# Lane steps, row loads and evacuation places of a hybrid encoder layer, on one core

## Chip, core and metric

The kernel runs on one core of one Trainium2 chip. The metric is the device time in microseconds (us) of one execution, as the median over runs. The core's engines are TensorE (PE, with its weight loads PEld), VectorE (DVE), ScalarE (ACT), GpSimd (POOL) and SyncE (SP), which here issues nearly all DMAs.

## The reference

One layer of a bidirectional hybrid encoder, in float32, on two sequences with shared weights: 1024 tokens (sample) and 256 tokens (prompt), 2048 features, each with a memory of 256 rows.

```python
hn = rms_norm(x, norm_g)
proj = hn @ w_in                       # 2048 x 4896
xbc, z_ssd, dt_raw, q, k, v, z_att, mq, z_mem = split_cols(proj, IN_SIZES)
xbc = silu(centred_dwconv(xbc, conv_w, conv_b))          # 5 taps along the tokens
xs, Bm, Cm = split_cols(xbc, (1024, 256, 256))
dt = softplus(dt_raw + dt_bias); A = -exp(a_log)
y = ssd_scan(forward) + ssd_scan(backward) + d_skip * xs  # 16 heads of 64, chunks of 128
o_ssd = rms_norm(y * silu(z_ssd), per group of 512)
o_att = window_attention(rms_norm(q), rms_norm(k), v, sink) * silu(z_att)  # 8 heads of 64, 2 kv heads
mk, mv = split_cols(rms_norm(mem) @ w_mem_kv)
o_mem = softmax(rms_norm(mq) @ rms_norm(mk).T) @ mv * silu(z_mem)          # 4 heads of 128
return x + concat([o_ssd, o_att, o_mem]) @ w_out
```

In a chunk the scan needs exp(acs[i] - acs[j]) for all pairs of tokens i, j, with acs the running sums of dt * A; both directions share one weight matrix per head.

## The kernel before

The 1280 tokens are ten tiles of 128 (tiles 0 to 7 the sample, 8 and 9 the prompt), in two groups of five. The big products run one after the other as blocks: first the memory's keys and values (two blocks of four tiles), then for group 0 the blocks q, kv (with dt), za (gate of the attention), x (six blocks, followed by the convolution), mq, zm, z0 and z1, then group 1 in another order, then the output product for both groups. `block_tok` accumulates five token tiles over 16 slices of the contraction (a step is one slice), `block_feat` two feature chunks in two halves of 320 tokens. Each product is done in three passes on rounded numbers: the activations are kept as a high and a low part (xH, xL), and each weight slice is loaded by SP (wraw, four places), rounded on ScalarE (wh, L219 or L222) and its rest formed on VectorE (wl, L220 or L223), with three places each. When a block's accumulators (five banks, tile acc) are complete, an evacuation function takes them out: `ev_mk`, `ev_raw` and `ev_dtkv` copy through a tile with the tag "evu" (two places) and store to DRAM, the gates use "evt" for the tanh (th) and "evu" for the result (zs), the convolution "evu" for its input and "evt" for the rest.

Everything else is written as generators, the lanes. Two queues of generators take turns; `pump(n)` runs n steps, a step being the code up to the next `yield`. `run` gives a block's rate: so many lane steps per slice (the table RATES, one column for each group). `need` runs steps until a named generator is done. The lanes are: `x_stats` and `mem_stats` (sums of squares of the rows of x and of the memory, tiles xst and mst, then the reciprocal root), `vectors` (small parameters; aneg is -exp(a_log)), `mk_prep`, `k_prep`, `attn` and `mem_attn` (load a tile that an evacuation stored, square it on ScalarE, sum on VectorE, `rsqrt`, multiply on VectorE, transpose on TensorE, then scores and values), `dt_prep` (running sums, stored to the tensor ac), `ssd_up` (forward sweep of the scan, and the weights within a chunk) and `ssd_down` (backward sweep). `rsqrt` is two instructions of GpSimd, L133 (scale and EPS) and L134 (power -0.5).

In `ssd_up`, `weights(q)` makes the weight matrices of four heads: rows of running sums are loaded from ac to all 128 partitions (rf forward, two places; rb backward, three places), ScalarE adds a bias per head (L848, eight instructions), VectorE merges both (copy_predicated, L849), ScalarE takes the exponential (L850) and VectorE multiplies (L851); `diag` uses the matrices on TensorE. The first product of a tile's `ssd_up` is pcb (L775), on the chunks that the convolution stored (bc).

The order on each engine is not the order of the source alone: a scheduler takes instructions by priority (the place in the source; weight splits and evacuations are moved up by high_priority) as soon as it expects their inputs and places to be ready. The queues themselves run in order on the chip.

Of the kernel before, what the change touches and what calls it, by code (L numbers as in the profile page):

```python
# [10 lines left out]
F32 = mybir.dt.float32  # L11
# [8 lines left out]
P = 128  # L20
# [7 lines left out]
SCR = 1024  # L28
CH, WB, RB, WA, WBB = 3, 3, 4, 5, 4
RBB = 3  # L30
RATES = ({'kv': 1.7, 'q': 1.5, 'za': 1.5, 'x': 1.5, 'mq': 2.52, 'zm': 1.8, 'z0': 2.17, 'z1': 1.26},
         {'kv': 0.84, 'x': 1.35, 'z0': 3.81, 'z1': 2.6, 'q': 2.65, 'za': 0.93, 'mq': 2.9, 'zm': 2.54,
          'o': 2.6})
NEG = -1e30

C_X, C_Z, C_DT, C_Q, C_K, C_V, C_ZA, C_MQ, C_ZM = 0, 1536, 2560, 2592, 3104, 3232, 3360, 3872, 4384
# [4 lines left out]
def hymba_encoder_kernel(  # L41
# [24 lines left out]
    ev = ctx.enter_context(tc.tile_pool(name="ev", bufs=2))  # L66
# [65 lines left out]
    def rsqrt(dst, src, scale, n):  # L132
        G.tensor_scalar(out=dst, in0=src, scalar1=scale, scalar2=EPS, op0=ALU.mult, op1=ALU.add)  # L133
        G.tensor_tensor(out=dst, in0=dst, in1=mhalf[:, :n], op=ALU.pow)  # L134
# [201 lines left out]

    def ev_raw(dst, base):
        def f(i, ps):
            z = ev.tile([P, 512], F32, tag="evu", name="qs")
            A.activation(z, ps, AF.Copy)  # L340
            S.dma_start(dst[base + i], z)
        return f

    def ev_dtkv(base):
        def f(i, ps):
            t = base + i
            rt = rx[:, t:t + 1]
            r = ev.tile([P, P], F32, tag="evu", name="kraw")
            A.activation(r, ps[:, 32:160], AF.Copy, scale=rt)
# [56 lines left out]
    def w2(name):  # L406
        return mp.tile([P, 512], F32, tag="wa", name=name, bufs=WA)

    def ev_mk(i, ps):
        kr = ev.tile([P, 512], F32, tag="evu", name="mkr")  # L410
        A.activation(kr, ps, AF.Copy)
        S.dma_start(mq_d[i], kr)

# [8 lines left out]
    def mk_prep(i):  # L422
        kr = w2("mkr")
        S.dma_start(kr, mq_d[i])
        ss = sm.tile([P, 4], F32, tag="s4", name="ss", bufs=4)
        sq = w2("sq")
        rm = rx[:, 10 + i:11 + i]
        A.activation(sq, kr, AF.Square, scale=rm)
        V.reduce_sum(out=ss, in_=hv(sq, 4), axis=AX.X)
        r = sm.tile([P, 4], F32, tag="s4", name="r", bufs=4)  # L430
        rsqrt(r, ss, 1.0 / P, 4)
        V.scalar_tensor_tensor(out=hv(kr, 4), in0=hv(kr, 4), scalar=rm, in1=hb(r, 4, P), op0=ALU.mult, op1=ALU.mult)
        V.tensor_mul(hv(kr, 4), hv(kr, 4), gm.unsqueeze(1).broadcast_to([P, 4, P]))
        for _ in range(4):
            yield
        ps = psum("pmk")
        for h in range(4):
            T.transpose(ps[:, h * P:(h + 1) * P], kr[:, h * P:(h + 1) * P], ident)
        c = slice((i % 2) * P, (i % 2) * P + P)
        if i < 2:  # L440
            A.activation(mkH[:, :, c], hv(ps, 4), AF.Copy)
            V.tensor_sub(mkL[:, :, c], hv(ps, 4), mkH[:, :, c].bitcast(F32))
        else:
            o = w2("mko")
            A.activation(o, ps, AF.Copy)
            S.dma_start(mk_d[:, :, c], hv(o, 4))
        yield
# [13 lines left out]
    def k_prep(t):  # L461
        r = w2("kr")[:, :P]
        S.dma_start(r, k_d[t])
        ss = sm.tile([P, 2], F32, tag="s2", name="kss", bufs=4)
        sq = w2("ksq")[:, :P]
        A.activation(sq, r, AF.Square)
        V.reduce_sum(out=ss, in_=hv(sq, 2), axis=AX.X)
        rr = sm.tile([P, 2], F32, tag="s2", name="krr", bufs=4)
        rsqrt(rr, ss, 1.0 / 64, 2)
        r3 = hv(r, 2)  # L470
        V.tensor_mul(r3, r3, hb(rr, 2, 64))
# [87 lines left out]
    def attn(t):  # L559
# [7 lines left out]
        tc_ = slice(ti * P, (ti + 1) * P)  # L567
        q = w2("q")
        S.dma_start(q, q_d[t])
        sq = w2("sq")  # L570
        A.activation(sq, q, AF.Square, scale=rx[:, t:t + 1])
        ss = sm.tile([P, 8], F32, tag="s8", name="qss", bufs=4)
        V.reduce_sum(out=ss, in_=hv(sq), axis=AX.X)
        r = sm.tile([P, 8], F32, tag="s8", name="qr", bufs=4)
        rsqrt(r, ss, 1.0 / 64, 8)
        q3 = hv(q)
        V.scalar_tensor_tensor(out=q3, in0=q3, scalar=rx[:, t:t + 1], in1=hb(r, 8, 64), op0=ALU.mult, op1=ALU.mult)
        yield
        yield
        yield  # L580
        qT = []
        for b in range(2):
# [12 lines left out]
        z = w2("za")  # L595
# [70 lines left out]
    def mem_attn(t):  # L666
        grp, ti = divmod(t, 5)
        tc_ = slice(ti * P, (ti + 1) * P)
        q = w2("mq")
        S.dma_start(q, mq_d[t])  # L670
        sq = w2("sq")
        A.activation(sq, q, AF.Square, scale=rx[:, t:t + 1])
        ss = sm.tile([P, 4], F32, tag="s4", name="mss", bufs=4)
        V.reduce_sum(out=ss, in_=hv(sq, 4), axis=AX.X)
        r = sm.tile([P, 4], F32, tag="s4", name="mr", bufs=4)
        rsqrt(r, ss, 1.0 / P, 4)
        q3 = hv(q, 4)
        V.scalar_tensor_tensor(out=q3, in0=q3, scalar=rx[:, t:t + 1], in1=hb(r, 4, P), op0=ALU.mult, op1=ALU.mult)
        yield
        yield  # L680
        yield
        ps = psum("pmq")
        for h in range(4):
# [5 lines left out]
        z = w2("zm")  # L689
# [68 lines left out]
    def ssd_up(t):  # L758
# [6 lines left out]
        for g in range(2):  # L765
            x = wb("xc", shape=(P, 4, P))
            S.dma_start(x, xbc_d[4 * g:4 * g + 4, :, tok].rearrange("f p c -> p f c"))
            xc.append(x)
        yield
        yield  # L770
        yield

        ps = psum("pcb")
        for g in range(2):
# [26 lines left out]
        for g in range(2):  # L801
# [22 lines left out]
            if not first:  # L824
# [4 lines left out]
                S.dma_start(sb_d[t][:, c], st)  # L829
                yield  # L830
        mts = {}

        def weights(q):
            g = q // 2

            rf = mp.tile([P, 512], F32, tag="rf", name="rf", bufs=2)
            mt = mp.tile([P, 512], F32, tag="rb", name="rb", bufs=RBB)
            r0 = 32 * (t % 5) + 4 * q
            for d, r in enumerate((rf, mt)):
                S.dma_start(r, ac_d[t // 5][r0 + 16 * d:r0 + 16 * d + 4, :]  # L840
                            .rearrange("h c -> (h c)").partition_broadcast(P))
            yield

            for d, r in enumerate((rf, mt)):
                for j in range(4):
                    c = slice(j * P, (j + 1) * P)
                    h = 16 * d + 4 * q + j
                    A.activation(r[:, c], r[:, c], AF.Identity, bias=wj_all[:, t, h:h + 1])  # L848
            V.copy_predicated(hv(mt, 4), upper.bitcast(U32).unsqueeze(1).broadcast_to([P, 4, P]), hv(rf, 4))  # L849
            A.activation(mt, mt, AF.Exp)  # L850
            V.tensor_mul(hv(mt, 4), hv(mt, 4), cb[:, g, :].unsqueeze(1).broadcast_to([P, 4, P]))  # L851
            mts[q] = mt

        def diag(g):
# [9 lines left out]
            V.tensor_add(ya[g], ya[g], py)  # L864
            S.dma_start(yp_d[t][:, g * 512:(g + 1) * 512], ya[g])

        for q in range(3):
            yield from weights(q)
            yield
        diag(0)  # L870
        yield
        yield from weights(3)
        yield
        yield
        diag(1)
# [136 lines left out]
    def vectors(_):  # L1012
        gk, gmk = w2("gk")[:, :64], w2("gmk")[:, :P]
        for t, a in ((gq, q_norm_g[0]), (gk, k_norm_g[0]), (gm, mq_norm_g[0]), (gmk, mk_norm_g[0]),
                     (dskip, d_skip[0]), (sinkb, sink[0]), (dtb, dt_bias.rearrange("o a h -> (o a h)")),
                     (aneg, a_log.rearrange("o a h -> (o a h)"))):
            S.dma_start(t, a.partition_broadcast(P))
        yield
        yield
        yield  # L1020
        yield
        V.scalar_tensor_tensor(out=gq, in0=gq, scalar=64 ** -0.5, in1=gk, op0=ALU.mult, op1=ALU.mult)
        V.scalar_tensor_tensor(out=gm, in0=gm, scalar=P ** -0.5, in1=gmk, op0=ALU.mult, op1=ALU.mult)
        A.activation(aneg, aneg, AF.Exp)
        V.tensor_scalar(out=aneg, in0=aneg, scalar1=-1.0, scalar2=None, op0=ALU.mult)
        yield
# [153 lines left out]
```

## Time and profile before

| | |
|---|---|
| median of 3 runs | 1917.64 us (1916.83 to 1919.4) |
| profiled execution | 1925.01 us, span 1923.3 us |
| busy | PE 1875.9 us, DVE 1049.4 us, ACT 760.9 us, POOL 81.6 us |
| DMA | 289.40 MB, mean 150 GB/s |

The span is the time from the first to the last instruction in the profiled execution; that execution is the one with the profiler on. A row of the list of instructions in order of time reads: start, length, engine, line, operation, written tile<-read tiles, shapes, count, and in brackets the idle time of the engine just before and what ended it. A row of the list of waits reads: engine, tile and line that waited <- engine, tile and line that it waited for: total us, times, longest. L12 is line 12 of the kernel.

### The profile page before, as it was taken

The page shows a single profiled execution, that of the slowest core. Times are in us where ns is not written, and L with a number is a line of the kernel's source. Part 1 is how long each engine was busy: PE and PEld are TensorE (multiplying, and loading weights), DVE is VectorE, ACT ScalarE, POOL GpSimd, SP SyncE. Part 2 cuts the span into 40 slices and gives each one's busy share as a digit, 9 for nine tenths or more (in the row PEclk, how much of TensorE's full clock was granted, in tenths as well). Part 3 has the DMA queues.
Part 4 walks back from the last instruction along what each step waited for, and adds up shares of the span by engine and source line. Part 5 has one row for each costly group of instructions (what it writes and reads, how often), then busy time and mean ns, then how long its engine had stood idle before and what let it go on. Part 6 is the DMA issues. An engine that isn't in the chain of part 4 may idle for free.

```text
span 1923.3 us, 28675 instructions
## 1 busy us (share of the span) xinstructions
PE 1875.9 (98%) x10568; PEld 1634.2 (85%) x10568; DVE 1049.4 (55%) x2133; ACT 760.9 (40%) x1721; POOL 81.6 (4%) x147
## 2 busy tenths in 40 slices
PE   8999989999999999999999999999999999999999
PEld 6779989998898879999978778978978787778887
DVE  4443646677564555667776554576675454542222
ACT  6462463333452545423436444334453333421121
POOL 1010010000000000000100000000000000000000
PEclk9999999999999999999999999999999999999999
DMA  8683563233343545433444567655555345454432
GB/s 272 198 257 104 157 182 121 85 114 109 116 124 113 154 140 172 138 96 101 140 131 142 158 177 247 209 187 162 170 158 186 123 149 159 136 176 132 133 120 69
DMA packets 191340, 289.40 MB, mean 150 GB/s; under 512 B 18977, under 2 KB 68193, under 8 KB 191201
## 3 DMA queue, kind: packets, MB, share of 16 engines
q1 hardware_dynamic: 191056, 287.53, 48.9%
q8 instruction: 83, 1.36, 0.3%
q14 instruction: 57, 0.46, 0.1%
q10 hardware_dynamic: 144, 0.06, 0.0%
HBM read 230.59 MB, written 56.92 MB: 149 GB/s over the span
## 4 chain that ended last, share of the span: by engine, by line
PE 77%; DMA 11%; ACT 4%; DVE 4%; issue 2%; POOL 1%; SPq 1%; ACTq 0%; DVEq 0%; POOLq 0%
PE acc L269 14%; PE acc L270 14%; PE acc L271 14%; PE acc L304 8%; PE acc L305 8%; PE acc L306 8%; DMA xst<-in_x_sample_dram 2%; DMA rf<-ac 2%; PE po L648 2%; PE py L858 1%; PE ppt L637 1%; DMA rb<-ac 1%; DVE wl L220 1%; PE pst L826 1%; PE pst L817 1%
## 5 line engine op out<-in xcount | busy, mean ns | idle before, releaser
L269 PE MATMUL acc<-wh,xH 128*128 128x512 f32 (+1 forms) x1568 | 619.0, 395 | 9.0 <-ACT wh L219 5.6
L270 PE MATMUL acc<-wl,xH 128*128 128x512 f32 (+1 forms) x1568 | 601.6, 384 | 2.9 <-DVE wl L220 2.7
L271 PE MATMUL acc<-wh,xL 128*128 128x512 f32 (+1 forms) x1568 | 600.3, 383 | 0.0
L220 DVE TENSOR_TENSOR wl<-wraw,wh 128x512 fp32r<-128x512 f32 (+1 forms) x416 | 278.3, 670 | 384.4 <-ACT wh L219 376.1
L219 ACT ACTIVATE wh<-wraw 128x512 fp32r<-128x512 f32 (+1 forms) x416 | 254.1, 612 | 528.7 <-PE acc L271 268.0
L304 PE MATMUL acc<-xH,wh 128*128 128x320 f32 x1280 | 406.1, 317 | 9.0 <-DVE zs L331 4.7
L306 PE MATMUL acc<-xH,wl 128*128 128x320 f32 x1280 | 396.6, 310 | 1.6 <-DVE wl L220 1.4
L305 PE MATMUL acc<-xL,wh 128*128 128x320 f32 x1280 | 396.6, 310 | 0.0
L269 PEld LDWEIGHTS acc<-wh,xH 128*128 128x128 f32 x1568 | 296.4, 189 | 69.2 <-issue 8.4
L270 PEld LDWEIGHTS acc<-wl,xH 128*128 128x128 f32 x1568 | 296.7, 189 | 62.9 <-issue 6.6
L271 PEld LDWEIGHTS acc<-wh,xL 128*128 128x128 f32 x1568 | 296.2, 189 | 56.5 <-issue 0.6
L304 PEld LDWEIGHTS acc<-xH,wh 128*128 128x128 f32 x1280 | 241.3, 189 | 15.0 <-DVE zs L331 5.2
L305 PEld LDWEIGHTS acc<-xL,wh 128*128 128x128 f32 x1280 | 241.3, 189 | 3.3 <-issue 3.2
L306 PEld LDWEIGHTS acc<-xH,wl 128*128 128x128 f32 x1280 | 241.1, 188 | 2.3 <-DVE wl L220 2.3
L223 DVE SCALAR_TENSOR_TENSOR wl<-wraw,vec,wh 128x512 fp32r<-128x512 f32 x64 | 48.0, 750 | 128.0 <-ACT wh L222 128.0
L222 ACT ACTIVATE wh<-wraw,vec 128x512 fp32r<-128x512 f32 x64 | 46.3, 723 | 145.4 <-PE acc L271 132.3
L379 DVE SCALAR_TENSOR_TENSOR c<-u,vec,c 128x638 f32<-128x638 f32 (+1 forms) x96 | 84.5, 880 | 1.0
L848 ACT ACTIVATE rb<-rb,wj_all 128x128 f32<-128x128 f32 x160 | 53.0, 391 | 49.1 <-DMA rb<-ac 46.5
L848 ACT ACTIVATE rf<-rf,wj_all 128x128 f32<-128x128 f32 x160 | 53.6, 390 | 33.5 <-DMA rf<-ac 33.5
L622 ACT ACTIVATE lg<-lg,nm 128x384 f32<-128x384 f32 (+1 forms) x80 | 45.1, 564 | 46.2 <-DVE nm L616 46.1
L849 DVE COPY_PREDICATED rb<-upper,rf 128x512 f32<-128x512 uint32 x40 | 30.3, 757 | 53.0 <-ACT rb L848 52.8
L214 DVE SCALAR_TENSOR_TENSOR xL<-chd,vec,xH 128x640 fp32r<-128x640 f32 (+1 forms) x48 | 39.6, 837 | 23.5 <-ACT xH L213 23.5
(238 smaller groups left out, 1725.5 us busy)
## 6 DMA issues: line engine op xcount, KB each, us to landing
wraw<-in_w_in_laid_dram SPq DMA_DIRECT2D x288, 256.0 KB, 2.8
wraw<-in_w_out_laid_dram SPq DMA_DIRECT2D x128, 256.0 KB, 2.7
chd<-in_x_turned_dram SPq DMA_DIRECT2D x32, 320.0 KB, 4.1
rf<-ac SPq DMA_DIRECT2D x40, 256.0 KB, 3.8
rb<-ac SPq DMA_DIRECT2D x40, 256.0 KB, 4.2
out_dram<-yt SPq DMA_DIRECT2D x40, 256.0 KB, 3.6
wraw<-in_w_mem_laid_dram SPq DMA_DIRECT2D x32, 256.0 KB, 4.3
xst<-in_x_sample_dram SPq DMA_DIRECT2D x32, 256.0 KB, 4.9
```

What stands on the lines that cost most here:

```text
L219: A.activation(h, raw, AF.Copy)
L220: V.tensor_sub(l, raw, h.bitcast(F32))
L222: A.activation(h, raw, AF.Copy, scale=g)
L223: V.scalar_tensor_tensor(out=l, in0=raw, scalar=g, in1=h.bitcast(F32), op0=ALU.mult, op1=ALU.subtract)
L269: T.matmul(ps[t][:, :n], sh, h[:, :n], start=(k_ == 0), stop=False)
L270: T.matmul(ps[t][:, :n], sh, l[:, :n], start=False, stop=False)
L271: T.matmul(ps[t][:, :n], sl, h[:, :n], start=False, stop=(k_ == KT - 1))
L304: T.matmul(o, sh, cur["H", q][:, m, c], start=(k == 0), stop=False)
L305: T.matmul(o, sh, cur["L", q][:, m, c], start=False, stop=False)
L306: T.matmul(o, sl, cur["H", q][:, m, c], start=False, stop=(k == KT - 1))
L379: V.scalar_tensor_tensor(out=c[:, :n], in0=u[:, k:k + n], scalar=cw[k], in1=c[:, :n], op0=ALU.mult, op1=ALU.add)
L848: A.activation(r[:, c], r[:, c], AF.Identity, bias=wj_all[:, t, h:h + 1])
```

## The change

Four things change in the source.

- In `mk_prep`, `k_prep`, `attn` and `mem_attn` a yield is added behind the load, and one or two between `rsqrt` and the multiplication that uses it; yields behind the multiplication are taken out, so that `attn` and `mem_attn` (of which the first is shown) keep their number of steps, `mk_prep` has one more and `k_prep` two. `vectors` waits six steps instead of four for its loads, with one more before the exponential of a_log.
- In `ssd_up` the loads of the rows are taken out of `weights(q)` into `rows(q)`, which is called a step ahead; for tiles 0 and 4 six yields stand behind the first loads instead of three.
- `ev_raw`, `ev_dtkv` and `ev_mk` (the first is shown) take their tile from "evt" for odd tiles and from "evu" for even ones.
- All rates are set anew.

```diff
-RATES = ({'kv': 1.7, 'q': 1.5, 'za': 1.5, 'x': 1.5, 'mq': 2.52, 'zm': 1.8, 'z0': 2.17, 'z1': 1.26},
-         {'kv': 0.84, 'x': 1.35, 'z0': 3.81, 'z1': 2.6, 'q': 2.65, 'za': 0.93, 'mq': 2.9, 'zm': 2.54,
-          'o': 2.6})
+RATES = ({'kv': 1.8, 'q': 1.7, 'za': 1.7, 'x': 1.7, 'mq': 2.7, 'zm': 1.9, 'z0': 2.4, 'z1': 1.6},
+         {'kv': 1.0, 'x': 1.4, 'z0': 3.7, 'z1': 2.8, 'q': 2.8, 'za': 1.3, 'mq': 2.8, 'zm': 2.4,
+          'o': 2.65})
...
     def ev_raw(dst, base):
-            z = ev.tile([P, 512], F32, tag="evu", name="qs")
+            z = ev.tile([P, 512], F32, tag="evt" if i % 2 else "evu", name="qs")
...
     def mk_prep(i):
         S.dma_start(kr, mq_d[i])
+        yield
...
         rsqrt(r, ss, 1.0 / P, 4)
+        yield
+        yield
         V.scalar_tensor_tensor(out=hv(kr, 4), in0=hv(kr, 4), scalar=rm, in1=hb(r, 4, P), op0=ALU.mult, op1=ALU.mult)
         V.tensor_mul(hv(kr, 4), hv(kr, 4), gm.unsqueeze(1).broadcast_to([P, 4, P]))
-        for _ in range(4):
-            yield
+        yield
+        yield
...
     def k_prep(t):
         S.dma_start(r, k_d[t])
+        yield
...
         rsqrt(rr, ss, 1.0 / 64, 2)
+        yield
         r3 = hv(r, 2)
...
     def attn(t):
         S.dma_start(q, q_d[t])
+        yield
...
         rsqrt(r, ss, 1.0 / 64, 8)
+        yield
         q3 = hv(q)
         V.scalar_tensor_tensor(out=q3, in0=q3, scalar=rx[:, t:t + 1], in1=hb(r, 8, 64), op0=ALU.mult, op1=ALU.mult)
-        yield
-        yield
         yield
...
     def ssd_up(t):
-        yield
-        yield
-        yield
+        for _ in range(6 if t in (0, 4) else 3):
+            yield
...
-        def weights(q):
-            g = q // 2
+        def rows(q):
             rf = mp.tile([P, 512], F32, tag="rf", name="rf", bufs=2)
             mt = mp.tile([P, 512], F32, tag="rb", name="rb", bufs=RBB)
...
-            yield
+            rows_[q] = rf, mt
+
+        def weights(q):
+            g = q // 2
+            rf, mt = rows_.pop(q)
...
+        rows(0)
+        yield
         for q in range(3):
-            yield from weights(q)
+            if q < 2:
+                rows(q + 1)
+                yield
+            weights(q)
             yield
         diag(0)
-        yield
-        yield from weights(3)
+        rows(3)
+        yield
+        yield
+        weights(3)
...
     def vectors(_):
-        yield
-        yield
-        yield
-        yield
+        for _ in range(6):
+            yield
         V.scalar_tensor_tensor(out=gq, in0=gq, scalar=64 ** -0.5, in1=gk, op0=ALU.mult, op1=ALU.mult)
         V.scalar_tensor_tensor(out=gm, in0=gm, scalar=P ** -0.5, in1=gmk, op0=ALU.mult, op1=ALU.mult)
+        yield
         A.activation(aneg, aneg, AF.Exp)
```

More of the change, by code (lines that the diff above doesn't have):

```diff
@@ L347, in f @@
             rt = rx[:, t:t + 1]
-            r = ev.tile([P, P], F32, tag="evu", name="kraw")
+            r = ev.tile([P, P], F32, tag="evt" if i % 2 else "evu", name="kraw")
             A.activation(r, ps[:, 32:160], AF.Copy, scale=rt)
@@ L409, in ev_mk @@
     def ev_mk(i, ps):
-        kr = ev.tile([P, 512], F32, tag="evu", name="mkr")
+        kr = ev.tile([P, 512], F32, tag="evt" if i % 2 else "evu", name="mkr")
         A.activation(kr, ps, AF.Copy)
@@ L831, in ssd_up @@
         mts = {}
-        def weights(q):
-            g = q // 2
+        rows_ = {}
+        def rows(q):
             rf = mp.tile([P, 512], F32, tag="rf", name="rf", bufs=2)
@@ L1017, in vectors @@
             S.dma_start(t, a.partition_broadcast(P))
-        yield
-        yield
-        yield
-        yield
+        for _ in range(6):
+            yield
         V.scalar_tensor_tensor(out=gq, in0=gq, scalar=64 ** -0.5, in1=gk, op0=ALU.mult, op1=ALU.mult)
         V.scalar_tensor_tensor(out=gm, in0=gm, scalar=P ** -0.5, in1=gmk, op0=ALU.mult, op1=ALU.mult)
+        yield
         A.activation(aneg, aneg, AF.Exp)
```

## Prediction

> **What bounds the kernel now.** I read the page first: busy times and the chain.
>
> ```profile
> span 1923.3 us, 28675 instructions
> PE 1875.9 (98%) x10568; PEld 1634.2 (85%) x10568; DVE 1049.4 (55%) x2133; ACT 760.9 (40%) x1721; POOL 81.6 (4%) x147
> ...
> PE 77%; DMA 11%; ACT 4%; DVE 4%; issue 2%; POOL 1%; SPq 1%; ACTq 0%; DVEq 0%; POOLq 0%
> ```
>
> The view of cores has the clock:
>
> ```profile
> core 0: 1923.3 us, clock 0.994
> ```
>
> TensorE is the bound. It is idle for 1923.3 - 1875.9 = 47.4 us, and the mean granted clock, 0.994, costs (1 - 0.994) x 1923.3, some 11.5 us more. No change that leaves the matmuls alone can win more than about 59 us, and this one leaves them alone: the built orders hold the same products, with lane steps moved between them. So I looked for where the 59 us are lost, with the view that gives busy time by stretches. Columns: stretch, length, busy time of PE, PEld, DVE, ACT, POOL with instruction counts, granted clock, DMA share, GB/s.
>
> ```profile
> 55.00:70.00 15.00, 11.62 (x39) 9.13 (x38) 3.55 (x6) 4.24 (x8) 0.00 (x0) 0.77 0.48 159
> 255.00:270.00 15.00, 10.56 (x57) 10.26 (x56) 7.21 (x18) 10.97 (x32) 2.08 (x4) 0.77 0.57 180
> 285.00:300.00 15.00, 12.52 (x82) 11.93 (x82) 10.88 (x23) 6.60 (x16) 0.00 (x0) 1.00 0.44 123
> 975.00:990.00 15.00, 12.59 (x66) 10.08 (x65) 10.50 (x24) 4.45 (x11) 0.00 (x0) 1.00 0.40 112
> 1395.00:1410.00 15.00, 13.63 (x84) 11.96 (x82) 10.45 (x20) 8.07 (x17) 0.00 (x0) 0.89 0.60 197
> 1410.00:1425.00 15.00, 13.20 (x70) 10.45 (x69) 9.89 (x29) 10.29 (x32) 0.00 (x0) 1.00 0.74 233
> 1620.00:1635.00 15.00, 12.36 (x50) 9.83 (x50) 7.55 (x12) 3.74 (x6) 1.20 (x2) 0.89 0.92 301
> 1725.00:1900.00 175.00, 175.00 (x774) 144.91 (x773) 47.15 (x67) 35.50 (x52) 0.00 (x0) 1.00 0.40 120
> ```
>
> The last row is TensorE without lanes: 774 products in 175 us, 0.226 us each, nothing lost. A step of block_tok with five row tiles is 15 products, 3.4 us: the rhythm at which ScalarE must deliver a weight split (wh) and VectorE its rest (wl). The first two rows lose most: 15 - 11.62 = 3.4 us idle and 0.23 x 15 = 3.45 us of clock, and 4.4 idle and 3.45 of clock. Two places hold a quarter of all that can be won.
>
> **The lanes' extra steps.** What the added yields do is decided by the scheduler, so I laid the built orders of the two kernels side by side. The waits that the yields are meant to cover:
>
> ```profile
> DVE q L577 <- POOL qr L134: 15.8, 8, 3.2
> DVE mq L678 <- POOL mr L134: 12.3, 10, 1.4
> DVE kr L471 <- POOL krr L134: 9.6, 9, 2.0
> DVE mkr L432 <- POOL r L134: 5.4, 4, 1.4
> ACT rb L848 <- DMA rb<-ac: 46.5, 23, 4.8
> ACT rf L848 <- DMA rf<-ac: 33.5, 23, 4.3
> ACT xst L928 <- DMA xst<-in_x_sample_dram: 15.6, 13, 3.8
> ACT xst L928 <- DMA xst<-in_x_prompt_dram: 11.6, 6, 3.3
> ```
>
> (Columns: total us, times, longest.) The first four rows are 43.1 us in 31 waits, 1.4 each. In the order before, 18 of the 34 users of such an rsqrt stand directly behind the reduction on VectorE; in the changed order still 13. A user is put into the queue as soon as its inputs are expected, whatever step it was written in. So 5 x 1.4 = 7 us of VectorE's waits go. Queued behind such a wait is wl, and three weight tiles are kept, so only a part reaches TensorE. All rows above are 43.1 + 80.0 + 27.2 = 150.3 us; if TensorE's whole 47.4 us of idleness came from them, 0.32 of a wait would reach it. That is the end on one side, 0 the other, and I take the middle, 0.16: -1.1 here, of 0 to -2.2.
>
> For the rows of running sums I counted how many of the weight loads that SP has issued ahead are still unused when ScalarE first uses a row: on average 2.71 before and 2.64 after, over 80 loads. The load is issued when its place is free, and that was so before. 0.07 of a 3.4 us step is 0.25 us more cover, against 80.0 us of waits in 46 places, 1.74 each: 46 x 0.25 = 11.7 us of ScalarE's time, 0.16 of it -1.9. Queued behind these waits on ScalarE is wh. On SP the load now waits for the copy_predicated of one step ago, not two, and weight loads queue behind it; they have four places, over 10 us of lead, so I put that at nothing. Taken apart, rb's lead grows by 0.22 of a step (0.77 us x 23 waits x 0.32 = -5.6) and rf's falls by 0.08 (0.26 x 23 x 0.32 = +1.9); these are the bounds.
>
> **Two sets of places for the evacuations.**
>
> ```profile
> 56.56 0.23 ACT L1024 ACTIVATE aneg<-aneg 128x32 f32<-128x32 f32 x1 [5.01 <-DMA aneg<-in_a_log_dram]
> 57.98 0.60 ACT L411 ACTIVATE mkr<-acc 128x512 f32<-128x512 f32 x1 [1.19 <-DMA mq<-mkr]
> ```
>
> These are two rows of ScalarE's instructions in order of time (start, length, in brackets the idle time before and what ended it). Four rows of the list of waits go with them:
>
> ```profile
> PEld acc L269 <- ACT mkr L411: 3.8, 1, 3.8
> ACT kraw L349 <- DMA k<-kraw: 2.1, 4, 0.9
> PEld acc L304 <- ACT kraw L349: 0.9, 1, 0.9
> PE pcb L775 <- DMA bc<-xbc_d: 3.2, 2, 2.4
> ```
>
> At 55 us TensorE waits for an accumulator that ScalarE empties late. ScalarE stands 5.01 us at aneg's load, which has two more steps and a yield in the source; but in the changed order the load is SP's entry 58 as before, and the exponential stands between the second and the third evacuation, as before. That wait stays. The 1.19 us behind it, for the store that frees a place, goes: -1.2 (nothing if the store was no later than the weights; -6.8, the stretch's whole loss, if the load were early by luck). For kraw the same: -0.9, of 0 to -2.1.
>
> The first tiles of each group's scan (6 steps of lead in place of 3): the first pcb stands 24.5 us of products behind the last one of the convolution, where it was 16.0; the second one 16.9, where it was 17.4. The row has two waits, the longer 2.4; that one (975:990) stays, the other 0.8 goes: -0.8.
>
> **Rates and the order that follows.** The rates shift steps between blocks; no matmul is added, so their own cost is nothing, and what counts is which work stands ahead of a block's last evacuation. The stall at 256 us, by VectorE's instructions in order of time:
>
> ```profile
> 253.70 0.88 DVE L331 TENSOR_TENSOR zs<-acc,rbc 128x320 f32<-128x320 f32 x2
> 256.72 0.73 DVE L849 COPY_PREDICATED rb<-upper,rf 128x512 f32<-128x512 uint32 x1 [2.14 <-ACT rb L848]
> 257.35 0.82 DVE L333 SCALAR_TENSOR_TENSOR zs<-th,zs 128x640 f32<-128x640 f32 x1
> 258.09 0.28 DVE L467 TENSOR_REDUCE kss<-ksq 128x2 f32<-128x128 f32 x1
> 258.36 0.69 DVE L220 TENSOR_TENSOR wl<-wraw,wh 128x512 fp32r<-128x512 f32 x1
> 259.94 0.29 DVE L471 TENSOR_TENSOR kr<-kr,krr 128x128 f32<-128x128 f32 x1 [0.89 <-POOL krr L134]
> 260.15 0.88 DVE L331 TENSOR_TENSOR zs<-acc,rbc 128x320 f32<-128x320 f32 x2
> ```
>
> and in the same view, TensorE's product that it held up and three of ScalarE's instructions ahead of it:
>
> ```profile
> 260.69 0.63 PE L304 MATMUL acc<-xH,wh 128*128 128x320 f32 x1 [4.43 <-DVE zs L331]
> ...
> 254.76 0.63 ACT L928 ACTIVATE xst<-xst 128x512 f32<-128x512 f32 x1 [0.88 <-POOL rx L134]
> ...
> 256.59 0.72 ACT L332 ACTIVATE th<-zs 128x640 f32<-128x640 f32 x1
> ...
> 257.71 0.61 ACT L219 ACTIVATE wh<-wraw 128x512 fp32r<-128x512 f32 x1
> ```
>
> The second half's zs (L331) came 6.45 us after the first, behind the rows' copy_predicated, a key's reduction and the wait for its rsqrt. In the changed order only L333 and one wl stand between the two; on ScalarE the tanh, one square of x_stats and one wh. That chain is 0.88 + 0.72 + 0.63 + 0.61 + 0.69 = 3.5 us, and with a wait for the square's load (15.6 / 13 = 1.2) 4.7. So the stall falls by 6.45 - 4.7 = 1.7 us, to 2.7. The clock: 2.6 us idle cost 0.11 x 15 = 1.65 us in 1620:1635, so 1.8 of the 3.45 come back. Term: -3.5; bounds -7.9 (all of it) and +1 (the load's longest wait, 3.8, in place of 1.2, less what is won).
>
> [...]
>
> Around 1395 to 1425 the rows of token tile 8 fell together with the refill of the output quads (349th to 352nd weight split): their first uses stand at the 351st to 357th split before, at the 342nd to 347th after, so they are done when the refill begins. Lost there: 1.4 + 1.65 of clock + 1.8 = 4.8; I take half, -2.4, of 0 to -4.8. Against it: the twenty later squares of x_stats stand within splits 76 to 90 before, nineteen within 77 to 87 after, so their loads come closer together. 285:300 lost 2.5 that way; I take 0, of -2.5 to +5.
>
> **Sum.** -1.1 - 1.9 - 1.2 - 0.9 - 0.8 - 3.5 - 2.4 = -11.8 us. The profiled execution took 1925.0 us (span 1923.3), so 1913.2 there. The median of the unprofiled runs, 1917.64, is 7.4 lower for the same work, so 1905.8.
>
> **The rivals.** *Only the places count* (0.20): the scheduler hides steps and rates alike, since 13 of 34 users still follow their reduction and the rows' lead is unchanged; what is left is -1.2 - 0.9 - 0.8 = -2.9, 1914.7, inside the 0.2% (3.8 us) that a measurement of this kernel can tell from no change. Against it: the order around the gates and the refill did change.
>
> *Loads of x collide with the evacuations* (0.24), the one on the slower side: the squares, packed into four splits fewer, each stand on ScalarE ahead of a tanh or a wh. Their loads already wait 27.2 us in 19 places. If two waits beyond the 2.7 us of stall above fall before the evacuation at 256 us and at the next block's start, each makes another stall of 4.4 us with 3.45 of clock: 2 x 7.9 - 11.8 + 3.5 (the term not won) = +7.5, 1925.1. It decides from about two such stalls.
>
> *All of it works* (0.10): the rows' end (-5.6), both worst stretches (-6.8, -7.9), the refill (-4.8) and the rest (-2.2 - 0.9 - 0.8) go: -29, 1888.6. For it: ScalarE and VectorE are at 40% and 55%. Against it: aneg stands where it stood.
>
> **Numbers.** The forecast has 0.46, the likeliest, so 1905.8. With its two largest terms at their ends (-7.9 and -4.8, or +1 and 0) it runs from 1899.0 to 1912.7; with the rows at -5.6 as well, to 1895.3. To leave out no more than 2 in 10 the range goes from 1895 to 1925, just short of the slower case with both stalls. Faster by over 0.2%: 0.42 of the forecast's 0.46, 0.07 of the second case, all of the last: 0.59. Within: 0.04 + 0.13 = 0.17. Slower: 0.24.
>
> **What would show it.** Right: L411 and L349 without a store in front; the aneg wait still near 5 us; rb and rf waits still 60 us or more together; VectorE's waits for POOL at L134 near 36 us; the zs stall below 3 us; granted clock above 0.994. Wrong: waits of xst above 35 us, or a new stretch at half clock after 255 us; or rb and rf below 40 us together, which would mean that the earlier load does what the order does not show.

## The result, and the profile after

The changed kernel takes 1916.48 us in the median of 20 runs (1913.77 to 1922.75). The kernel before, run beside it, takes 1922.62 us in 20 runs (1912.25 to 1927.8); the first three of these are the ones shown ahead of the prediction, and their median of 1917.64 us was at the low side. The medians are 6.1 us apart, the means (1921.9 and 1917.1) 4.8. The ratio, which goes by the means, is 0.9975, with a 95% interval of 0.9964 to 0.9986: the change is faster, by 4.8 us, where 11.8 us were forecast. The measured time lies in the forecast's range of 1895 to 1925 us, but so does the kernel before, so the range says little.

Below, a ratio or a difference of two ratios is turned into us by 1922: a kernel at 0.9902 is (0.9975 - 0.9902) x 1922 = 14.0 us below the changed one. The experiments ran in four groups, and each ratio is to the before of its own group, 17 to 23 runs. In the second group (steps with rates, the two kernels with waits left out, aneg) before's median was 1915.24 us, in the others 1921.5 to 1923.1; no run shows why. A difference to the changed kernel, which was measured apart from all four, has an error of 3 to 4 us from the two intervals.

The page of the changed kernel and its view of cores:

```profile
span 1914.9 us, 28709 instructions
PE 1876.0 (98%) x10568; PEld 1631.8 (85%) x10568; DVE 1055.0 (55%) x2133; ACT 761.7 (40%) x1721; POOL 83.5 (4%) x147
...
PE 78%; DMA 10%; DVE 5%; ACT 3%; issue 2%; POOL 1%; SPq 1%; ACTq 0%; DVEq 0%
```

```profile
core 0: 1914.9 us, clock 0.997
```

TensorE's idle time is 1914.9 - 1876.0 = 38.9 us, from 47.4, and the clock is 0.997, from 0.994. The stretches that the prediction looked at, by the view of busy time in stretches (length, busy time of PE, PEld, DVE, ACT, POOL, granted clock, DMA share, GB/s). Work comes 3 us earlier in the first two, so they start 3 us earlier; the fifth, new, is shown with before's row for the same time under the list:

```profile
52.00:67.00 15.00, 12.95 (x57) 10.07 (x56) 3.55 (x6) 4.07 (x9) 0.00 (x0) 1.00 0.55 181
252.00:267.00 15.00, 11.40 (x69) 11.10 (x69) 6.12 (x17) 7.56 (x20) 2.52 (x5) 0.89 0.75 223
285.00:300.00 15.00, 15.00 (x106) 14.99 (x105) 13.10 (x23) 4.58 (x8) 2.41 (x2) 1.00 0.28 86
975.00:990.00 15.00, 14.79 (x70) 11.09 (x69) 10.46 (x21) 3.27 (x6) 0.00 (x0) 1.00 0.23 64
1371.00:1386.00 15.00, 12.38 (x82) 11.53 (x81) 13.00 (x29) 9.34 (x21) 0.00 (x0) 0.89 0.53 158
1395.00:1410.00 15.00, 15.00 (x86) 12.56 (x87) 11.72 (x22) 5.92 (x11) 0.00 (x0) 1.00 0.70 240
1410.00:1425.00 15.00, 14.80 (x80) 12.21 (x79) 9.31 (x17) 5.49 (x10) 0.00 (x0) 1.00 0.71 228
1622.00:1637.00 15.00, 11.49 (x57) 9.77 (x57) 5.91 (x10) 2.47 (x4) 1.57 (x2) 0.89 0.76 222
```

```profile
1371.00:1386.00 15.00, 15.00 (x115) 14.63 (x114) 7.87 (x13) 7.06 (x15) 0.00 (x0) 1.00 0.77 218
```

At 1395 to 1425 us before lost 4.8 us and the changed kernel 0.2. But at 1371 to 1386 us it now loses 15 - 12.38 = 2.6 us idle and 0.11 x 15 = 1.65 us of clock, 4.3 in all, where before was busy throughout (and lost 1.35 us from 1380 to 1395): most of the loss moved 25 us ahead. At 1622 us it loses 3.5 + 1.65, about 0.9 us more than before at 1620.

The waits (total us, times, longest):

```profile
ACT rb L856 <- DMA rb<-ac: 54.9, 25, 4.5
ACT rf L856 <- DMA rf<-ac: 35.9, 27, 3.1
ACT xst L943 <- DMA xst<-in_x_sample_dram: 17.0, 14, 2.8
DVE q L584 <- POOL qr L134: 12.7, 8, 2.1
DVE kr L476 <- POOL krr L134: 11.4, 9, 2.0
DVE mq L685 <- POOL mr L134: 9.4, 9, 1.4
...
ACT xst L943 <- DMA xst<-in_x_prompt_dram: 5.6, 5, 2.2
ACT aneg L1038 <- DMA aneg<-in_a_log_dram: 5.4, 1, 5.4
DVE mkr L435 <- POOL r L134: 4.9, 4, 1.6
```

The four waits for GpSimd are 38.4 us, from 43.1. The rows' two are 90.8, from 80.0, although their loads are written a step earlier. The stores that mkr and kraw waited for are gone from the list; aneg's wait stays.

### The profile page after: what moved, and what is told of

It is laid out like the page before. It is cut to its first block, busy times and chain, and to the rows that moved or that the text cites. A ratio compares the mean times of both kernels' runs of the same rounds, so it can differ in the third digit from the quotient of the medians.

```text
span 1914.9 us, 28709 instructions
## 1 busy us (share of the span) xinstructions
PE 1876.0 (98%) x10568; PEld 1631.8 (85%) x10568; DVE 1055.0 (55%) x2133; ACT 761.7 (40%) x1721; POOL 83.5 (4%) x147
## 4 chain that ended last, share of the span: by engine, by line
PE 78%; DMA 10%; DVE 5%; ACT 3%; issue 2%; POOL 1%; SPq 1%; ACTq 0%; DVEq 0%
PE acc L269 15%; PE acc L270 15%; PE acc L271 15%; PE acc L304 7%; PE acc L306 7%; PE acc L305 7%; DMA xst<-in_x_sample_dram 2%; PE po L653 1%; DMA rb<-ac 1%; PE py L866 1%; DMA chd<-in_mem_turned_dram 1%; DVE wl L220 1%; PE ppt L642 1%; PE pmo L740 1%; PE pst L821 1%
```

## The experiments

Three theories. The forecast's: 0.16 of a wait reaches TensorE, the order acts at two named places (zs at 256 us, the refill at 1400 us), and places, steps and rows each add their share. *Only the places count*: all else is hidden. *The order as a whole*: what counts is which small waits happen to meet along the run, so that parts do not add and any small step in a rate moves the time.

### One part at a time

The second set of places alone:

```
-            r = ev.tile([P, P], F32, tag="evu", name="kraw")
+            r = ev.tile([P, P], F32, tag="evt" if i % 2 else "evu", name="kraw")
... (the same for qs and mkr)
```

> Before, with the second set of places alone (qs, kraw and mkr use the two tags in turn). TensorE's order is that of before. The forecast put 2.9 us on this part (mkr's evacuation 1.2, kraw 0.9, and 0.8 that was booked on the first pcb and belongs to the steps): so -2.1 us, ratio 0.9989, and no ScalarE wait of kraw or mkr on a store. Rival 'only the places count': the whole gain of the change, -4.8 us (0.9975). Rival 'the order decides': within 1 us of before.

Measured: 0.9987 (0.9973 to 1.0001), -2.5 us. Neither kraw nor mkr waits for a store any more. That is the size booked, though the interval just reaches no change.

The rows ahead alone (`rows` split from `weights`, called a step earlier):

> Before, with the rows of running sums issued a step ahead and nothing else. As compiled, each of the five engines' programs holds the same instructions in the same order as before, so this is also a measure of how far two builds of one order differ. The forecast booked 1.9 us on the rows' lead; from the order it is 0: ratio 1.000, rb and rf waits together within 5 us of before's 80.0. A rival in which the earlier load itself is the gain: -2 us or more, and rb and rf waits together under 65 us.

Measured: 0.9994 (0.9983 to 1.0006): nothing. The rows' waits are 47.8 + 31.0 us, before's 80.0 all but unchanged. Written a step earlier, each load still goes out when the scheduler finds its place free: SP's DMAs stand in before's order, load by load. This run teaches something else, since its order is before's:

```profile
core 0: 1914.8 us, clock 0.997
```

Its profiled execution is 8.5 us shorter than before's with the same instructions in the same order. In its trace TensorE ran at half clock for 6.8 us at 256 us and 3.4 us at 1622 us (granted 0.86 from 245 to 270 us, 0.93 from 1620 to 1645); in before's trace also for 6.8 us at 58 us and 3.4 us at 1403 us (granted 0.50 from 58 to 64.5 us and from 1403 to 1406). So the 8.4 us between the two profiles of the change say little by themselves; only repeated runs can size it.

The rates alone, and the added steps alone:

```
-RATES = ({'kv': 1.7, 'q': 1.5, ...
+RATES = ({'kv': 1.8, 'q': 1.7, ...
```

> Before, with the new rates alone: the order in which blocks and steps meet is changed, no step is moved away from its rsqrt. The forecast put the two largest terms on this order (the zs stall at 256 us -3.5, the refill at 1400 us -2.4): -5.9 us, 0.9969. Rival 'only the places count': 0. Rival 'the order decides, by luck of which waits meet': a difference of 2 to 6 us of either sign, with stalls of TensorE above 1.5 us at other places than in before and after, and not the sum of parts.

```
         rsqrt(rr, ss, 1.0 / 64, 2)
+        yield
... (and the other steps of the diff)
```

> Before, with the added steps alone (behind the loads, between rsqrt and its users, before pcb for tiles 0 and 4, and in the load of the vectors). Forecast: rsqrt cover -1.1, first pcb -0.8: -1.9 us, 0.9990, VectorE's waits for GpSimd at L134 down from 43 to about 36 us. Rival 'only the places count': 0, and those waits stay at 43. Rival 'the order decides': a difference of 2 to 6 us of either sign through stalls elsewhere, whatever those waits do.

Measured: the rates alone 1.0047 (1.0030 to 1.0064), +9.0 us; the steps alone 1.0082 (1.0066 to 1.0099), +15.8 us. Yet the steps do just what they were to do. Their waits for GpSimd are in this list 38.5 us, from 43.1:

```profile
DVE q L584 <- POOL qr L134: 12.7, 8, 2.1
DVE mq L685 <- POOL mr L134: 11.2, 9, 1.4
DVE kr L476 <- POOL krr L134: 10.5, 10, 1.6
...
DVE mkr L435 <- POOL r L134: 4.1, 3, 1.5
```

What they cost stands elsewhere. Two of TensorE's waits and ScalarE's and VectorE's instructions in order of time, all of the steps alone:

```profile
PE ppt L642 <- DVE lg L632: 7.8, 4, 5.4
PE psc L612 <- ACT qT L598: 3.6, 2, 3.3
```

```profile
1266.77 0.69 ACT L852 ACTIVATE rf<-rf,wj_all 128x128 f32<-128x128 f32 x2 [2.50 <-DMA rf<-ac]
1267.37 0.60 ACT L627 ACTIVATE lg<-lg,nm 128x384 f32<-128x384 f32 x1
...
1268.06 0.60 ACT L627 ACTIVATE lg<-lg,nm 128x384 f32<-128x384 f32 x1
```

```profile
1268.78 0.16 DVE L629 TENSOR_TENSOR den<-den,es 128x2 f32<-128x2 f32 x1 [2.96 <-ACT lg L627]
...
1269.99 0.74 DVE L632 TENSOR_SCALAR lg<-lg,den 128x384 f32<-128x384 f32 x2
```

A row of running sums landed 2.5 us late, an attention tile's exponentials (lg) stood behind it on ScalarE, VectorE's reciprocal and scaling behind those, and TensorE, whose next instruction in line was the transpose of lg, stood 5.4 us with 6.8 us of half clock around it. None of the added steps stands at either place in the source: the new order put them next to each other. The wait of psc, at 1480 us, has another 6.8 us of half clock beside it. The rates alone have a like meeting at 531 us, where pT (L638) stands on ScalarE behind an evacuation of qs, two weight splits and a row that came 0.8 us late, and TensorE waits 3.1 us for it.

Both together, without places and rows:

> Before, with the added steps and the new rates together; one set of places, rows as before. Its order is the changed kernel's but for some 30 places on ScalarE and VectorE. If the parts add up, the two alone (+9.0 and +15.8 us) give +24.8 us. If the order as a whole decides, steps and rates were tuned to each other and the pair gives what is left of the change after the places: -4.8 + 2.5 = -2.3 us (0.9988), and neither the 3.3 us stall at 535 us of the rates alone nor the 5.6 us stall at 1270 us of the steps alone is there.

Measured: 0.9986 (0.9973 to 0.9998), -2.7 us, and of the two meetings neither is in its trace. The parts do not add: +9.0 and +15.8 make -2.7. With the places' -2.5 this fits the change's -4.8, within the errors.

### What a wait is worth

The rows' loads left out:

```
-            for d, r in enumerate((rf, mt)):
-                S.dma_start(r, ac_d[t // 5][...].partition_broadcast(P))
...
-                    A.activation(r[:, c], r[:, c], AF.Identity, bias=wj_all[:, t, h:h + 1])
+                    A.activation(r[:, c], rbc[:, c], AF.Identity, bias=dskip[:, h % 16:h % 16 + 1])
```

> The changed kernel without the 80 loads of the rows: the exponents' sums are taken from a constant tile with another bias, so the decay weights are not the reference's; all else is computed. Measures what share of ScalarE's 90.8 us of waits on rf and rb reaches TensorE. By the forecast's middle share of 0.16: -14.5 us against the changed kernel (0.990 against before); by its upper end of 0.32: -29 us. Rival 'TensorE is covered by three weight tiles': -5 us or less. Where only the stalls listed in the changed kernel's profile count, none of those above 1.5 us has a wait for rf or rb ahead of it: -3 us.

Measured: 0.9902 (0.9885 to 0.9919), 14.0 us below the changed kernel. Of 90.8 us of waits, 14.0 / 90.8 = 0.15 reached TensorE (0.11 to 0.20 by the intervals; or less, since 80 transfers went too): the forecast's share. Most of it is not in large stalls. The changed kernel's six stalls of TensorE above 1.5 us, none with a row directly ahead of it, are 15.6 us together, and those of this kernel still 10.4; the rest of the 14 us, as far as single profiles can say, is made of smaller ones. Its page:

```profile
span 1896.0 us, 28528 instructions
PE 1869.8 (99%) x10568; PEld 1632.4 (86%) x10568; DVE 1057.0 (56%) x2133; ACT 763.6 (40%) x1721; POOL 80.1 (4%) x147
```

TensorE is idle for 26.2 us, from 38.9.

The waits for rsqrt taken away, with the instructions left as they are:

```
-        V.tensor_mul(r3, r3, hb(rr, 2, 64))
+        V.tensor_mul(r3, r3, hb(dskip[:, :2], 2, 64))
... (the same for q, mq, mkr)
```

> The changed kernel, in which the users of the four rsqrt on GpSimd read a constant instead of its result: the normalising factors of q, k, mq and mk are left out, the instructions are the same and VectorE waits for GpSimd there no more. Measures what is left in the 38.4 us of these waits. Share 0.16: -6.1 us against the changed kernel; the row order theory, by which a wait of 1 to 2 us counts only where another stands beside it (248 to 251 us, 280 us, 1371 us, 1632 us): -4 us; fully covered: within 1 us.

Measured: 0.9902 (0.9886 to 0.9918), also 14.0 us below the changed kernel. That is 0.36 of the 38.4 us (0.26 to 0.47 by the intervals), more than twice the forecast's share; whether it is above its upper end of 0.32 the intervals leave open. Neither kernel owes its gain to a new order of TensorE: its products stand in the changed kernel's order at all but 67 (without rows) and 13 (here) of 10568 positions, though without rows ScalarE's order differs at 669 of 1721. The waits of this kernel show one reason: the wait is handed on. ScalarE's waits for the key and query that VectorE scales behind the rsqrt were, in the changed kernel,

```profile
ACT qh L590 <- DVE q L584: 18.7, 8, 3.7
ACT kh L481 <- DVE kr L477: 17.7, 9, 3.3
```

and are here

```profile
ACT qh L590 <- DVE q L584: 12.0, 7, 3.5
...
ACT kh L481 <- DVE kr L477: 7.4, 7, 2.3
```

so 17 us of ScalarE's waits go with VectorE's 38.4, and both engines have weight splits queued behind.

Aneg's load first among the vectors:

```
-        for t, a in ((gq, q_norm_g[0]), ...
-                     (aneg, a_log.rearrange("o a h -> (o a h)"))):
+        for t, a in ((aneg, a_log.rearrange("o a h -> (o a h)")), (gq, q_norm_g[0]), ...
```

> The changed kernel with aneg's load issued first among the vectors instead of last. TensorE's order is untouched. The 5.4 us wait of ScalarE on that load ends and with it the stall of 2.2 us at 58 us: -2 us against the changed kernel, and no half-clock stretch at 58 us in any run (up to 3.4 us more in those that had one), so -2 to -4 us (0.9955 to 0.9965 against before). Rival: the evacuation of mkr then waits for the next weights' split in its place, and the stall stays above 1.5 us: within 1 us.

Measured: 0.9955 (0.9940 to 0.9970), 3.8 us below the changed kernel, as expected, if just clear of the error. ScalarE's wait for the load is gone and TensorE's order is the same. The stretch that lost 6.8 us before and 2.1 in the changed kernel's profile is full:

```profile
52.00:67.00 15.00, 15.00 (x68) 12.43 (x67) 6.37 (x9) 6.96 (x11) 0.00 (x0) 1.00 0.61 193
```

### The place at 257 us

Squares of token tiles 5 to 9 from a constant, without their 20 loads:

```
-            A.activation(xt, xt, AF.Square, accum_out=s4[:, c:c + 1])
+            A.activation(xt, xt if t < 5 else rbc[:, :512], AF.Square, accum_out=s4[:, c:c + 1])
```

> The changed kernel, in which the squares of token tiles 5 to 9 (the 20 taken after 120 us) read a constant tile instead of a row of x: their 20 loads are left out, so the row scales of those tiles are not the reference's. TensorE's order is untouched. If the stall that the evacuation zs causes at 257 us (3.8 us, with half clock behind it) comes from ScalarE's wait of 2.1 us for x, it falls below 1.5 us and the small ones at 251 and 282 us go: -3.8 + 1.5 - 1.7 - 3.5 = -7.5 us against the changed kernel (0.9935 to 0.994 against before). If it comes from the many instructions that stand in line there (tanh, square, weight splits), as the kernel without the rsqrt waits hints (3.7 us still), it stays above 3 us: -3 us or less.

Measured: 0.9942 (0.9925 to 0.9959), 6.3 us below the changed kernel, near the expected 7.5; but the stall falls only from 3.8 to 2.7 us and still has 3.4 us of half clock beside it. With the load gone, VectorE's wait for a key's rsqrt and ScalarE's two kh are the next in line there. Part of the 6.3 us is therefore not from the stall.

The same squares queued later:

```
-    queue(1, x_stats, range(5, 10))
     need(x_rows, [0])
     gate_att(0)
+    queue(1, x_stats, range(5, 10))
```

> The changed kernel with the squares of token tiles 5 to 9 queued behind the first gates instead of ahead of them. Same work, all of it. If their place beside the first gates makes the stall at 257 us, it falls under 2 us and the time by 3 to 6 us against the changed kernel (0.994 to 0.996 against before), unless a like stall comes up later in the convolution, where the steps then are. If the order decides by luck: within 5 us either way, with the stalls elsewhere.

Measured: 1.0002 (0.9990 to 1.0014), 5.2 us above the changed kernel. The stalls at 251 and 254 us are down to 2.0 and 1.6 us, and the loss is back at 290 us, where ScalarE waits 4.38 us for a row of x, the convolution's u stands behind it, and TensorE behind that:

```profile
PE acc L304 <- DVE u L363: 5.3, 1, 5.3
```

A load moved away from one block's evacuation met the next one's.

### A load moved, and a rate by a tenth

Aneg's load first, and mq's load for the last tile two steps earlier:

```
         turn_(1)
+        if t == 8:
+            mq_next[9] = w2("mq")
+            S.dma_start(mq_next[9], mq_d[9])
         yield
```

> The changed kernel with aneg's load first (as in the run before) and the load of mq for the last token tile issued two steps before the end of the tile ahead of it, instead of after it. In the changed kernel that load is issued at 1623.0 us, ScalarE waits 6.4 us for it, and TensorE stalls 3.7 us and then runs 3.4 us at half clock. All of it: -3.7 - 1.7 = -5.4 us against the kernel with aneg first (0.9955), so 0.9927. If rsqrt and its two neighbours fill the time anyway, -1 to -2 us (0.9945 to 0.995).

Measured: 0.9941 (0.9924 to 0.9957). The stall at 1632 us, 2.8 to 4.0 us in most of these kernels, is no longer there, and the longest wait for that load falls from 6.4 to 4.1 us. But against aneg alone it is only 2.7 us, well inside the two intervals.

```
-'mq': 2.7
+'mq': 2.6
```

> The changed kernel with one rate of seventeen moved back by a step that means nothing (mq 2.7 to 2.6 in the first group; before had 2.52). If the time hangs on which waits happen to meet, as the steps and rates alone suggest, it moves by 2 us or more, to either side, by stalls that come or go behind 300 us. If the rates act only through the places that they were chosen for (zs at 257 us and the refill at 1400 us, neither of which this touches): within 1 us of the changed kernel (0.997 to 0.998 against before).

Measured: 0.9928 (0.9909 to 0.9947), 9.0 us below the changed kernel: this step, which fits no theory of a named place, brings almost twice what the whole change did. So I moved other rates: mq to 2.8; z1 of the second group from 2.8 to 2.7; and in the kernel before, mq from 2.52 to 2.42.

> The changed kernel with the rate mq of the first group at 2.8 in place of 2.7 (the run before had 2.6, and took 0.9928 of before). If the rate as such has a best value below 2.7, this is slower than the changed kernel by some us (0.999 to 1.002 against before) and 2.7 lies on a slope. If the order is a matter of luck, it is anywhere within 0.993 to 1.005, and its stalls above 1.5 us behind 500 us are others than the changed kernel's. A null effect (0.997 to 0.998) would say that 2.6 was a single lucky case.

> The changed kernel with the rate z1 of the second group at 2.7 in place of 2.8; TensorE's order is the same up to its 5704th product, so all before some 1100 us is untouched, the stall at 257 us too. By luck of the order: 2 us or more to either side of 0.9975, by stalls that come or go after 1100 us. By named places alone: within 1 us, unless the refill at 1400 us moves (then up to 4.8 us).

> The kernel before with its rate mq of the first group at 2.42 in place of 2.52, nothing else. By luck of the order: 2 us or more to either side of before (below 0.999 or above 1.001), so that the change's own -4.8 us is no more than such a step can bring. By named places: 1.000.

Measured: 0.9988 (0.9973 to 1.0004), 2.5 us above the changed kernel, which is within the error; 0.9929 (0.9916 to 0.9942), 8.8 us below; 1.0015 (1.0005 to 1.0025), 2.9 us above before. A lower rate is faster in two of these kernels and slower in a third. With z1 at 2.7 the stall at 257 us is still there (3.2 us, and 3.4 us of half clock); two late stretches tell where the time goes. The changed kernel:

```profile
1350.00:1395.00 45.00, 41.61 (x299) 38.77 (x297) 32.24 (x69) 23.99 (x54) 2.32 (x2) 0.96 0.55 160
1615.00:1645.00 30.00, 26.49 (x136) 22.31 (x135) 13.72 (x29) 8.93 (x22) 1.57 (x2) 0.94 0.58 172
```

and with z1 at 2.7:

```profile
1350.00:1395.00 45.00, 43.11 (x325) 40.92 (x324) 34.79 (x73) 27.37 (x68) 1.84 (x2) 1.00 0.61 186
1615.00:1645.00 30.00, 27.88 (x151) 23.16 (x151) 14.89 (x30) 11.05 (x23) 1.57 (x2) 1.00 0.58 179
```

Idle time falls by 1.5 + 1.4 us there, and the clock stays whole, worth 0.04 x 45 + 0.06 x 30 = 3.6 us: together 6.5 of the 8.8, as far as single profiles can say. With mq at 2.8 both stretches are better still (44.37 and 29.97 us busy), but at 1182 us, in the trace of that kernel, TensorE's pyb waits 3.7 us for VectorE's yd, which it does not in the changed kernel's trace.

All that helped, together: aneg, mq's load, and the rate at 2.6.

> The changed kernel with aneg's load first, mq's load for the last tile two steps earlier, and the rate mq at 2.6. Known causes add: aneg -3.9 and mq -2.7 us on top of the rate's 0.9928 give -20 us (0.9895). Since the rate alone has already half of the stall at 1632 us (1.9 against 3.7 us, no half clock), mq's share may be 1 us: 0.9905. Rival: each kernel's waits meet anew, and the gains do not add: 0.992 to 0.995.

Measured: 0.9913 (0.9899 to 0.9928), -16.7 us: faster than before and than the changed kernel by 11.9 us, less than the sum of the three (-20), and not to be told from the rate alone.

```profile
1615.00:1645.00 30.00, 29.99 (x152) 24.75 (x152) 13.46 (x27) 10.73 (x22) 1.20 (x2) 1.00 0.55 176
```

## Why the prediction was right in direction and wrong in size

By its terms, in its order:

- **rsqrt cover, -1.1.** The waits fell to 38.4 us (about 36 were expected). At the share that the kernel without them shows, 0.36, 4.7 us less wait would be worth -1.7. So the term was a little small, because the share was too low by more than half. No run measures the term by itself: the steps alone cut these waits as much (38.5 us) and cost 15.8 us by other ones.
- **The rows' lead, -1.9.** Nothing: the rows alone leave the order as it is and the time too, and in the full change's profile the waits are 10.8 us longer (not always: 80.7 us with aneg first, in the same order of TensorE). The step that failed is the 0.25 us of cover taken from a count of weight loads. The share of 0.16 on which it was priced came out (0.15), by luck: it was the middle between 0 and 0.32, taken for the waits for rsqrt as well, and those have 0.36.
- **Places, -1.2 and -0.9.** Right in mechanism, and in size as far as the interval tells: -2.5 us measured, 2.1 booked, with the stores' waits gone and aneg's wait left (5.4 us in the full change, 2.2 with the places alone).
- **The first pcb, -0.8.** That its wait would go was right. That the second one (975 to 990 us) would stay was wrong: the stretch lost 2.4 us before and 0.2 after, and with the steps alone pcb does not wait for bc either.
- **zs at 256 us, -3.5.** Mis-sized. The chain was built as forecast, with its wait for x at 2.1 us and not 1.2:

```profile
251.18 0.88 DVE L331 TENSOR_TENSOR zs<-acc,rbc 128x320 f32<-128x320 f32 x2
...
252.86 0.83 DVE L333 SCALAR_TENSOR_TENSOR zs<-th,zs 128x640 f32<-128x640 f32 x1 [0.81 <-ACT th L332]
256.18 0.69 DVE L220 TENSOR_TENSOR wl<-wraw,wh 128x512 fp32r<-128x512 f32 x1 [2.49 <-ACT wh L219]
256.79 0.88 DVE L331 TENSOR_TENSOR zs<-acc,rbc 128x320 f32<-128x320 f32 x2
```

```profile
254.91 0.63 ACT L943 ACTIVATE xst<-xst 128x512 f32<-128x512 f32 x1 [2.07 <-DMA xst<-in_x_sample_dram]
```

From zs to zs it takes 5.6 us, not 4.7 (before: 6.45). Four profiles with before's order at this place (before, places, rows, mq at 2.42) have stalls of 4.6, 5.5, 4.2 and 5.5 us, mean 4.9; eight with the changed one (the change, steps with rates, aneg, aneg with mq's load, mq at 2.6 and 2.8, z1 at 2.7, all together) have 3.8, 3.8, 4.0, 3.4, 3.9, 3.9, 3.2 and 3.9, mean 3.7. That is -1.2 us where -1.7 was taken. The clock was to bring 1.8 more; over the same profiles half clock lasted 6.0 us on average and then 4.7, and half of the difference is 0.6. So the term was -1.8. The sign that was named for it, a stall below 3 us, did not come.

- **The refill at 1400 us, -2.4.** It came in full where it was put (4.8 us lost before, 0.2 after), although 1.65 of the 4.8 was a half-clock stretch that two more profiles of that order of TensorE (places alone, rows alone) do not have near 1400 us. It was given back ahead of it, above all at 1371 to 1386 us, where the attention's po now waits for pT. TensorE's product, and what stands ahead of it on VectorE and ScalarE:

```profile
1375.98 1.25 PE L653 MATMUL po<-pT,v_all 128*64 128x128 f32 x12 [2.46 <-ACT pT L643]
```

```profile
1370.90 0.75 DVE L584 SCALAR_TENSOR_TENSOR q<-q,rx,qr 128x512 f32<-128x512 f32 x1 [1.73 <-POOL qr L134]
1371.58 0.15 DVE L623 TENSOR_TENSOR es<-sinkb,nm 128x2 f32<-128x2 f32 x1
```

```profile
1371.76 0.20 ACT L624 ACTIVATE es<-es 128x2 f32<-128x2 f32 x1 [1.76 <-DVE es L623]
...
1375.46 0.84 ACT L643 ACTIVATE pT<-ppt 128x384 f32<-128x384 f32 x2
```

VectorE waits 1.73 us for a query's rsqrt, the attention's es stands behind that multiplication, ScalarE waits 1.76 us for es, and pT follows behind nine more instructions. In the kernel without the waits for rsqrt ScalarE runs the same instructions here in the same order, without that wait, and po's longest wait is 0.7 us. So a wait that the steps were meant to cover now stands in front of another of TensorE's operands. Taking as lost the time by which TensorE's products start later than the median for their kind, 1325 to 1450 us lost 13.4 us in before's trace and 13.7 in the changed kernel's. This is the term that failed most: the prediction looked at what the new order takes away and not at where the moved steps arrive.

The granted clock rose above 0.994 as named (0.997), but so it did in the profile of the rows alone, whose order is before's.

So the steps and the rates, priced at -7.8 us together, brought -2.7; and the rows nothing of 1.9. Two places that were booked at nothing won besides (2.5 us at 285 us, 2.2 at 975 us), so more was given back than at 1376 us; apart from 0.9 us at 1622 us it was not followed where. A further 5.0 us of the error in the forecast's absolute time (1905.8 against 1916.48) is the three runs that it started from: 1917.64, against 1922.62 in twenty.

Of the rivals, *Only the places count* came nearest in time (-2.9 forecast) and is wrong in its reason: steps and rates are not hidden, they move the time by 9 and 16 us when taken alone. *Loads of x collide* did not decide here (the waits of xst fell to 22.6 us, no stall above 2 us in the next block), but it is what the kernel with the later squares shows. The sign that was named for it, a new stretch at half clock after 255 us, did appear, at 1378 us, with another cause. *All of it works* is refuted.

That the order as a whole decides is shown as far as this: of six edits of rates or yields, none of which adds or removes work, five moved the time, by -9.0 and -8.8 us (one rate of the changed kernel), by +2.9 (one rate of before) and by +9.0 and +15.8 (all rates, all steps), and the sixth by +2.5 within the error, each time with other stalls in the trace. For +9.0 and +15.8 a stall and what stands ahead of it were found; for -9.0 none that accounts for it (the stall at 1632 us is down from 3.7 to 1.9 us). Whether a good order can be foreseen from the built programs stays open.

## What to carry to other kernels

In this kernel, where an engine at 98% is fed by engines at 40% and 55%, on which a late operand holds up what is queued behind it (5.4 us of ScalarE at aneg's load), a change of yields or rates had no price of its own: do one part at a time, and try small steps in a rate before crediting a change with its intent, since a tenth in one rate was worth more here than the change. Price a wait by taking it away (0.15 of ScalarE's waits for rows, 0.36 of VectorE's waits for rsqrt reached TensorE), not by a share of all idle time. What can be planned is a load that an engine stands for in front of TensorE's next operand: aneg's, issued first, brought its 3.8 us.

## What the runs showed of the hardware

In these traces half clock comes, up to TensorE's last product, in stretches of 3.4 us or a multiple (6.8, once 10.2): in before's 6.8 us at 58 and at 259 us and 3.4 us at 1403 and at 1632 us, in the changed kernel's 3.4 us at 258, 1378 and 1634 us. In before's first one the granted clock is 0.50, and the 128x512 products start 0.43 us apart, against 0.23 behind it. Below 3 us the length of a stall alone does not tell whether such a stretch stands beside it. Over 18 profiled kernels, with a stall taken as the time by which TensorE's next product started later than the median for its kind, all 29 stalls above 3 us have such a stretch beside them (it begins between 5 us before and 4 us after the stall's end), 22 of 27 between 2.2 and 3 us, and 7 of 40 between 1.7 and 2.2 us (one or two more or fewer, by how kinds are told apart). A stall of 2.8 us at 59 us has none in the kernel with the rows alone (granted 1.00 from 43 to 68 us), one of 3.5 us has 6.8 us of half clock beside it in before's trace, at the same place in the same order.

Part of the scatter of one kernel's runs goes with the mean granted clock: across the 23 runs of before that stood beside the first four experiments (1915.84 to 1927.22 us, 0.993 to 0.998), a clock lower by 0.001 goes with 1.7 us more time (correlation -0.6).
